# Another model of loads and of the way to TensorE in the planner that orders a diffusion trunk's instructions

## The chip, the cores and the metric

One core of one Trainium2 chip. The metric is the device time of one execution in microseconds (us); a difference is read from medians of several runs. PE is TensorE, DVE VectorE, ACT ScalarE, POOL GpSimd, SP SyncE, which issues the loads.

## The reference

A diffusion backbone of two layers over 256 latent tokens and 256 context tokens, 1024 channels wide. Each layer has four branches side by side, one output projection, and a squared-ReLU MLP; scales and shifts come from a conditioning vector (adaLN). Cut to one layer, for the latent tokens:

```python
sh1, sc1, g1, sh2, sc2, g2 = ada_mod(c, w_ada[l], b_ada[l])     # silu(c) @ w + b, split in 6
u = x * (1.0 + sc1) + sh1
p = split_proj(u @ w_in[l] + b_in[l])
y_a, y_b = local_branches(p, ...)        # 3-tap gated conv; 31-tap conv, layer norm, silu
y_c = diff_post(diff_latent(...), ...)   # differential attention: softmax1 - lam * softmax2
y_d = na_latent(..., rpb[l])             # 2-D neighbourhood attention with a position bias
y = sum_i sigmoid(gate_i) * (y_i @ wb[i] + bb[i])
x = layer_norm(ALPHA * x + g1 * (y @ w_o[l]), ...)
h = x * (1.0 + sc2) + sh2
x = layer_norm(ALPHA * x + g2 * (relu(h @ w_ff1[l]) ** 2 @ w_ff2[l]), ...)
```

The context tokens go through the same weights in layer 0; in layer 1 only their keys and values are needed.

## The kernel before

**Products.** Every weight is loaded once from HBM in units of 128 x 1024 float32, 512 KB (`raw`, 344 loads). ScalarE rounds a unit to `whi` (a copy in a shorter format, L373), VectorE makes the rest `wlo = raw - whi` (L380), and every product is three matmuls: high by high, high by low, low by high. The activations have the same two parts (`u`, `a`, `yc`, `pt`, `qk`). At the very start half units are used (`wh`, `wl`). On TensorE (L427) `mm` are the products of `u` with the input projection and with the MLP's first matrix, `f` those of the MLP's second, `br` and `wo` the branch and output projections, `S` scores, `o` attention outputs, `PT` transposes of the softmax `P` (L487), which VectorE copies to `pt`.

**The conditioning vectors.** The first ones (layer 0) are matmuls on loaded blocks `a` at the start. The others are computed while layer work runs, from about 300 to 520 us and from 680 to 960 us: `araw` units of 512 KB (80 loads) are multiplied and summed on VectorE into `sums` (L407, a unit is several instructions), TensorE adds the partitions up (`ada<-sums`), and a row `adrow` is transposed (`adT`) into `mod`. `bt` is the position bias of the neighbourhood attention (loads of 128 KB), `var` the variance of the conv branch's layer norm from sums of squares (`sum<-sum,sq`, `conf`).

**Buffers.** One pool of ten units holds at most 3 `raw`, 3 `whi`, 3 `wlo` and 2 `araw`; a load can start only when a buffer of its kind is free.

**The order.** Nothing of it is written by hand. The kernel's pieces are threads with a priority, and `Sched.run` is a list scheduler: it always takes the operation that can start first by its own clock, the higher priority among equals, and emits it to its engine's queue; `_rather` lets a more urgent one go first if it comes within a fraction of the chosen one's time. The chip's engines then execute their queues strictly in this order and wait by semaphores. The clock is made of each operation's cost and of `lat()`, the time from one engine's result to another's use (L153 to L161): 200 ns behind PE, TO_PE into PE, 128 to 205 between others. All loads are issued by SP from `dma()` (L416). In the planner a load occupies SP for its bytes over 355 per ns, at least 80 ns, and its data count as landed 2100 ns later. Operations that VectorE or ScalarE can do alike are handed out in the same step by who can start first.

Of the kernel before, what the change touches and what calls it, by code (L numbers as in the profile page):

```python
# [24 lines left out]
CAPS_S = {"qkv": 24, "P": 8, "bt": 3, "pt": 12, "y": 24}  # L25
FIRST = 5
ADA_PACE = 108
TO_PE = 300.0
MM = 13.3
PRIO_ADA = 27  # L30
PRIO_X = 60
# [9 lines left out]
LO_AFTER = {(DEPTH - 1, ("f1", 1)): ("z", DEPTH - 1, 0, 1)}  # L41
AHEAD = {"DVE": 0.3, "ACT": 0.3}
MARGIN = 20
CAPS_W = {"raw": 3, "whi": 3, "wlo": 3, "araw": 2}
CAPS_PS = {"main": 4, "att": 4, "ada": 1}
ALPHA = (2 * DEPTH) ** 0.25
# [41 lines left out]
class Buf:  # L88
    __slots__ = ("tile", "wt", "we", "rt", "re", "res")

    def __init__(self, tile, t=0.0, res=None):
        self.tile, self.wt, self.we, self.rt, self.re, self.res = tile, t, None, 0.0, None, res
# [58 lines left out]
class Sched:  # L151
    @staticmethod
    def lat(a, b):  # L153
# [5 lines left out]
        if "PE" in (a, b):  # L159
            return 200.0 if a == "PE" else TO_PE  # L160
        return 205.0 if "POOL" in (a, b) else 143.0  # L161

    def __init__(self):
        self.free = {}
        self.table = 0
        self.active = []
        self.seq = 0
        self.wake = deque()
        self.blocked = 0
# [75 lines left out]
    def _rather(self, best):  # L245
# [7 lines left out]
        for j, t in enumerate(self.active):  # L253
            if t[1] + MARGIN > prio:
                continue
# [8 lines left out]
    def run(self, everything):  # L264
        self._settle()
        while self.active:
            best = None
            for i, t in enumerate(self.active):
                op = t[3]
                for way in op[1]:  # L270
                    s = max(self.free.get(way[0], 0.0), self._ready(op, way[0]))
                    key = (s, t[1], t[2], s + way[1])
                    if best is None or key < best[0]:
                        best = (key, i, way)
            best = self._rather(best)
            (s, _, _, _), i, (eng, cost, fn, table) = best
            if eng == "PE" and s < COLD:
                cost *= 2
            if eng == "ACT" and table is not None and table != self.table:
                self.table = table  # L280
                cost += 1283.0
            t = self.active.pop(i)
            _, _, w, r, lag = t[3]
            fn()
            end = s + cost
            self.free[eng] = end
            for v in r:
                for b in v.bufs:
                    if end > b.rt:
                        b.rt, b.re = end, eng  # L290
            for v in w:
                for b in v.bufs:
                    b.wt, b.we = end + lag, eng
            self.wake.append((t, end))
            self._settle()
        if not everything.done:
            raise RuntimeError("the threads wait for each other")
# [9 lines left out]
class Kernel(Sched):  # L307
    def __init__(self, tc, es, aps):
# [7 lines left out]
        self.R = {  # L316
            "wt": Resource(big, "wt", [128, 1024], 10, CAPS_W),
            "pad": Resource(big, "pad", [128, 572], 4),
# [96 lines left out]

    def dma(self, out, in_, bytes_):  # L416
        nc, a = self.nc, self._a
        return self._op("SP", max(80.0, bytes_ / 355.0), lambda: nc.sync.dma_start(out=a(out), in_=a(in_)),
                        [out] if isinstance(out, V) else [], [in_], lag=2100.0)

    def mm(self, calls, w, r, cost):

# [1490 lines left out]
```

## Time and profile before

| | |
|---|---|
| median of 3 runs | 1617.65 us (1616.54 to 1618.89) |
| the profiled execution | 1620.5 us, of which the span from first to last instruction is 1618.7 |
| mean granted TensorE clock | 0.993 of full speed |
| PE busy | 1573.0 us, 97% |
| DVE busy | 1300.3 us, 80% |
| ACT busy | 879.6 us, 54% |
| mean DMA rate | 157 GB/s |

The rows quoted below come from the profiled execution. A row of the list of waits reads: engine, what it was about to write, its line, what ended the wait, then the sum of such waits, how many, and the longest. A row of a timeline reads: start, duration, engine, line, operation, output and inputs, size; in square brackets the idle time just before it and what ended it. A duration is longer than the distance to the next start, because instructions of an engine overlap a little. A row of stretches has each engine's busy time, then the granted clock and the DMA's share and rate.

### The profile page before, as it was taken

The numbers are of one execution on the slowest core, as the hardware profiler recorded it, in microseconds if no ns is written. First come the engines' busy times: TensorE is split into PE (matmuls) and PEld (weight loads), VectorE is DVE, ScalarE is ACT, GpSimd is POOL, SyncE is SP. The second block draws the span as 40 slices with busy tenths as digits, with TensorE's granted clock in tenths as the row PEclk, the third lists the DMA queues.
The fourth block names the chain that finished last, engine by engine and source line by source line (L and its number), as shares of the span: only waits on it lengthen the run. The fifth ranks groups of instructions, "written<-read, shape, count | busy, mean of one in ns | idle before, by whom it ended". The sixth has DMA issues, their size and how long they took to land. (4 is left out here: it accounts for less than half of the span.)

```text
span 1618.7 us, 22984 instructions
## 1 busy us (share of the span) xinstructions
PE 1573.0 (97%) x8688; PEld 1338.1 (83%) x8688; DVE 1300.3 (80%) x2192; ACT 879.6 (54%) x1425; POOL 12.5 (1%) x51
## 2 busy tenths in 40 slices
PE   7999999999999999999999999999999999989997
PEld 4878878887878888887887868888997999989997
DVE  3899999599999747987676794899999797765566
ACT  3465366455744644742523324667587686576553
POOL 0000000000000000000000000000000000000000
PEclk9999999999999999999999999999999999999999
DMA  9322222544454155455555643543443444735563
GB/s 371 112 68 83 98 79 78 166 159 152 145 191 157 65 171 193 137 195 182 188 171 184 234 147 130 177 167 106 144 151 116 144 157 166 251 131 190 192 224 110
DMA packets 80707, 254.30 MB, mean 157 GB/s; under 512 B 9028, under 2 KB 13892, under 8 KB 80596
## 3 DMA queue, kind: packets, MB, share of 16 engines
q1 hardware_dynamic: 80596, 252.84, 46.1%
q8 instruction: 68, 1.11, 0.3%
q14 instruction: 43, 0.35, 0.1%
HBM read 250.67 MB, written 2.13 MB: 156 GB/s over the span
## 5 line engine op out<-in xcount | busy, mean ns | idle before, releaser
L427 PE MATMUL mm<-u,whi 128*128 128x512 f32 (+1 forms) x3168 | 789.0, 340 | 1.5 <-ACT u L373 0.7
L427 PEld LDWEIGHTS mm<-u,whi 128*128 128x128 f32 x3168 | 547.7, 191 | 66.9 <-DVE u L380 2.4
L427 PE MATMUL mm<-u,wlo 128*128 128x512 f32 (+1 forms) x1584 | 535.5, 338 | 0.6 <-DVE wlo L380 0.6
L373 ACT ACTIVATE whi<-raw 128x1024 fp32r<-128x1024 f32 x335 | 353.8, 1057 | 332.1 <-DVE wlo L380 122.7
L380 DVE TENSOR_TENSOR wlo<-raw,whi 128x1024 fp32r<-128x1024 f32 x335 | 408.7, 1221 | 146.6 <-PE mm L427 67.5
L427 PEld LDWEIGHTS mm<-u,wlo 128*128 128x128 f32 x1584 | 302.6, 191 | 32.6 <-DVE wlo L380 0.8
L407 DVE SCALAR_TENSOR_TENSOR sums<-araw,cs,sums 128x512 f32<-128x512 f32 x280 | 195.9, 747 | 57.9 <-DMA araw<-in_w_ada 57.4
L427 PE MATMUL f<-whi,a 128*128 128x512 f32 (+1 forms) x760 | 236.7, 389 | 0.0
L427 PEld LDWEIGHTS f<-whi,a 128*128 128x128 f32 x760 | 142.3, 188 | 31.2 <-issue 2.5
L427 PE MATMUL f<-wlo,a 128*128 128x512 f32 (+1 forms) x380 | 147.5, 388 | 1.8 <-DVE wlo L380 1.8
L407 DVE SCALAR_TENSOR_TENSOR conf<-glu,sm,conf 128x512 f32<-128x512 f32 (+1 forms) x240 | 137.6, 614 | 0.8
L427 PEld LDWEIGHTS f<-wlo,a 128*128 128x128 f32 x380 | 71.4, 188 | 17.2 <-DVE wlo L380 3.2
L373 ACT ACTIVATE P<-S,st 128x512 f32<-128x512 f32 (+1 forms) x96 | 58.6, 615 | 16.4 <-DVE st L1187 15.7
L373 ACT ACTIVATE gth<-mm,hb 128x512 f32<-128x512 f32 (+1 forms) x64 | 37.0, 578 | 37.2 <-PE mm L427 37.1
L427 PE MATMUL wo<-whi,mg 128*128 128x512 f32 (+1 forms) x184 | 56.6, 382 | 0.0
L1187 DVE TENSOR_REDUCE st<-S 128x1 f32<-128x512 f32 (+1 forms) x96 | 55.0, 591 | 0.2
L427 PE MATMUL S<-qk 128*128 128x512 f32 (+1 forms) x192 | 48.7, 368 | 4.5 <-ACT qk L373 2.4
L373 ACT ACTIVATE qk<-ra 64x512 fp32r<-64x512 f32 (+1 forms) x62 | 35.0, 565 | 24.4 <-DVE ra L380 22.1
L373 ACT ACTIVATE a2f<-mm 128x512 f32<-128x512 f32 (+1 forms) x64 | 30.7, 482 | 32.0 <-PE mm L427 32.0
L373 ACT ACTIVATE bh<-br,hb 128x512 f32<-128x512 f32 (+1 forms) x64 | 36.1, 573 | 16.3 <-PE br L427 16.2
L373 ACT ACTIVATE P<-P,st 128x512 f32<-128x512 f32 (+1 forms) x42 | 26.5, 643 | 33.1 <-DVE st L1236 27.8
L380 DVE TENSOR_TENSOR a<-a2f,a 128x512 fp32r<-128x512 f32 (+1 forms) x64 | 35.4, 556 | 10.6 <-ACT a L373 9.9
(206 smaller groups left out, 1934.9 us busy)
## 6 DMA issues: line engine op xcount, KB each, us to landing
raw<-in_W SPq DMA_DIRECT2D x344, 512.0 KB
araw<-in_w_ada SPq DMA_DIRECT2D x80, 512.0 KB
a<-in_w_ada SPq DMA_DIRECT2D x32, 256.0 KB
bt<-in_rpb SPq DMA_DIRECT2D x32, 128.0 KB
row<-g SPq DMA_DIRECT2D x12, 256.0 KB
x<-in_x_t SPq DMA_DIRECT2D x8, 256.0 KB
row<-in_ln_g SPq DMA_DIRECT2D x8, 256.0 KB
row<-in_ln_b SPq DMA_DIRECT2D x8, 256.0 KB
```

What stands on the lines that cost most here:

```text
L373: lambda: nc.scalar.activation(out=out.ap, in_=in_.ap, func=func, **kw),
L380: return self._op(eng, cost, lambda: e.tensor_tensor(out=out.ap, in0=x.ap, in1=y.ap, op=op), [out], [x, y])
L407: return self._op("DVE", cost, lambda: nc.vector.scalar_tensor_tensor(out=out.ap, in0=x.ap, scalar=a(s), in1=y.ap, op0=op0, op1=op1), [out ...
L427: nc.tensor.matmul(out=out, lhsT=x, rhs=y, start=start, stop=stop, **kw)
L1187: yield self.dve(68 + 1.04 * nk, lambda: nc.vector.tensor_reduce(out=mx.ap, in_=S.ap, axis=AX.X, op=ALU.max, negate=True), [mx], [S])
```

## The change

The planner's model is changed in three numbers and two places; no operation of the kernel is. TO_PE goes from 300 to 500 ns: the planner counts a result of another engine as usable by TensorE 200 ns later than before. A load is modelled in three parts: SP is busy for 330 ns, then the bytes go one load after another through one path (`self.loads`) at 315 per ns instead of 355, then 2700 ns instead of 2100 pass until they count as landed. So in the planner SP is free for the next issue after 0.33 us, where a 512 KB load had held it for 1.48.

```diff
--- before.py
+++ after.py
@@ -25,7 +25,7 @@
 CAPS_S = {"qkv": 24, "P": 8, "bt": 3, "pt": 12, "y": 24}
 FIRST = 5
 ADA_PACE = 108
-TO_PE = 300.0
+TO_PE = 500.0
 MM = 13.3
 PRIO_ADA = 27
 PRIO_X = 60
@@ -41,6 +41,9 @@
 LO_AFTER = {(DEPTH - 1, ("f1", 1)): ("z", DEPTH - 1, 0, 1)}
 AHEAD = {"DVE": 0.3, "ACT": 0.3}
 MARGIN = 20
+DMA_LAG = 2700.0
+DMA_RATE = 315.0
+DMA_ISSUE = 330.0
 CAPS_W = {"raw": 3, "whi": 3, "wlo": 3, "araw": 2}
 CAPS_PS = {"main": 4, "att": 4, "ada": 1}
 ALPHA = (2 * DEPTH) ** 0.25
@@ -162,6 +165,7 @@
 
     def __init__(self):
         self.free = {}
+        self.loads = 0.0
         self.table = 0
         self.active = []
         self.seq = 0
@@ -282,8 +286,11 @@
             t = self.active.pop(i)
             _, _, w, r, lag = t[3]
             fn()
-            end = s + cost
-            self.free[eng] = end
+            if eng == "SP":
+                self.free[eng] = s + DMA_ISSUE
+                end = self.loads = max(s + DMA_ISSUE, self.loads) + cost
+            else:
+                end = self.free[eng] = s + cost
             for v in r:
                 for b in v.bufs:
                     if end > b.rt:
@@ -415,8 +422,8 @@
 
     def dma(self, out, in_, bytes_):
         nc, a = self.nc, self._a
-        return self._op("SP", max(80.0, bytes_ / 355.0), lambda: nc.sync.dma_start(out=a(out), in_=a(in_)),
-                        [out] if isinstance(out, V) else [], [in_], lag=2100.0)
+        return self._op("SP", bytes_ / DMA_RATE, lambda: nc.sync.dma_start(out=a(out), in_=a(in_)),
+                        [out] if isinstance(out, V) else [], [in_], lag=DMA_LAG)
 
     def mm(self, calls, w, r, cost):
```

What follows is order. TensorE and SP have as many instructions as before; VectorE has 14 more and ScalarE 14 fewer, since operations that either can do went to the other. Lines of the code below L164 stand four, those below L285 up to seven lines further down.

At the variance of the conv branch's norm (383 us in the trace of before), on TensorE, before and now:

```order
L427 MATMUL mm<-u,whi 128x512 x2
L427 MATMUL mm<-u,wlo 128x512
L427 MATMUL var<-sum,on_77 128x512
L487 MATMUL PT<-ident,P 128x128 x4
L427 MATMUL br<-yc,whi 128x512 x2
L427 MATMUL br<-yc,wlo 128x512
```

```order
L434 MATMUL mm<-u,whi 128x512 x2
L434 MATMUL mm<-u,wlo 128x512
L434 MATMUL var<-sum,on_77 128x512
L434 MATMUL mm<-u,whi 128x512 x2
L434 MATMUL mm<-u,wlo 128x512
```

`var` now stands 38 rows later on TensorE, in the midst of `mm` products; the `br` products that stood behind it are ahead of it now.

On VectorE at the same place, the last of the three sums of squares that `var` needs, before and now:

```order
L380 TENSOR_TENSOR sum<-sum,sq 128x512
L380 TENSOR_TENSOR conf<-conf,mu 128x512
L407 SCALAR_TENSOR_TENSOR gth<-gth,bh 128x512
L407 SCALAR_TENSOR_TENSOR sums<-araw,cs,sums 128x512
L380 TENSOR_TENSOR sum<-sum,sq 128x512
L380 TENSOR_TENSOR acc<-acc,gth 128x512
L380 TENSOR_TENSOR wlo<-raw,whi 128x1024
```

```order
L414 SCALAR_TENSOR_TENSOR sums<-araw,cs,sums 128x512 x2
L387 TENSOR_TENSOR wlo<-raw,whi 128x1024
L387 TENSOR_TENSOR S<-S,bt 128x256
L1194 TENSOR_REDUCE st<-S 128x1
L387 TENSOR_TENSOR sum<-sum,sq 128x512
L1243 RECIPROCAL st<-st 128x1
L394 TENSOR_SCALAR P<-P,st 128x512
```

The sum had a step of `gth` and one of `sums` just ahead of it; now it follows two `wlo`, a bias addition and a reduction, and the `sums` stand ahead of those.

On SP, the loads around the second pair of `bt` in this stretch (418 us in the trace of before), before and now:

```order
L418 DMA raw<-in_W 128x1024 x4
L418 DMA g_102<-adrow 1x512 x2
L418 DMA g_103<-adrow 1x512 x2
L418 DMA ba<-in_b_ada 128x1x512
L418 DMA araw<-in_w_ada 128x1024
L418 DMA bt<-in_rpb 128x256 x2
L418 DMA araw<-in_w_ada 128x1024 x2
L418 DMA raw<-in_W 128x1024
```

```order
L425 DMA raw<-in_W 128x1024
L425 DMA bt<-in_rpb 128x256 x2
L425 DMA raw<-in_W 128x1024 x2
L425 DMA g_102<-adrow 1x512 x2
L425 DMA g_103<-adrow 1x512 x2
L425 DMA ba<-in_b_ada 128x1x512
L425 DMA araw<-in_w_ada 128x1024 x4
L425 DMA raw<-in_W 128x1024 x2
```

The pair of `bt` stood behind the rows `g`, the bias `ba` and an `araw`; now it stands ahead of those and of two `raw`, and four `araw` stand in a row behind `ba`.

On VectorE in the MLP of layer 0, up to the `wlo` that ended at 932.67 in the trace of before and a little beyond it, before and now:

```order
L380 TENSOR_TENSOR a_8084<-a2f,a_8083 128x512
L407 SCALAR_TENSOR_TENSOR sums<-araw,cs,sums 128x512 x2
L380 TENSOR_TENSOR wlo<-raw,whi 128x1024
L407 SCALAR_TENSOR_TENSOR sums<-araw,cs,sums 128x512 x2
L380 TENSOR_TENSOR wlo<-raw,whi 128x1024
L407 SCALAR_TENSOR_TENSOR sums<-araw,cs,sums 128x512 x7
L380 TENSOR_TENSOR wlo<-raw,whi 128x1024
L407 SCALAR_TENSOR_TENSOR sums<-araw,cs,sums 128x512
L380 TENSOR_TENSOR wlo<-raw,whi 128x1024
```

```order
L387 TENSOR_TENSOR a_8062<-a2f,a_8061 128x512
L414 SCALAR_TENSOR_TENSOR sums<-araw,cs,sums 128x512 x2
L387 TENSOR_TENSOR wlo<-raw,whi 128x1024
L414 SCALAR_TENSOR_TENSOR sums<-araw,cs,sums 128x512 x5
L387 TENSOR_TENSOR wlo<-raw,whi 128x1024
L414 SCALAR_TENSOR_TENSOR sums<-araw,cs,sums 128x512 x3
L387 TENSOR_TENSOR wlo<-raw,whi 128x1024
L387 TENSOR_TENSOR yacc<-f_8036,yacc 128x512
L387 TENSOR_TENSOR yacc<-yacc,row 128x512
L414 SCALAR_TENSOR_TENSOR sums<-araw,cs,sums 128x512
```

The `wlo` in question is the one behind `sums` x7 before, and the one behind `sums` x3 now: four of the seven steps moved ahead of the `wlo` in front of it.

## Rows read from the trace of the kernel before

**Rows 1.** The page's first part: busy time of each engine, its share of the span, its instructions.

```profile
PE 1573.0 (97%) x8688; PEld 1338.1 (83%) x8688; DVE 1300.3 (80%) x2192; ACT 879.6 (54%) x1425; POOL 12.5 (1%) x51
```

**Rows 2.** The list of waits of TensorE, whole span, costliest first.

```profile
PE mm L427 <- ACT wh L373: 4.8, 2, 3.2
PE var L427 <- DVE sum L380: 3.7, 1, 3.7
...
PE ada L427 <- DVE sums L407: 2.4, 6, 0.7
...
PE f L427 <- DVE wlo L380: 1.8, 2, 1.6
PE adT L487 <- DVE adrow L380: 1.2, 2, 0.9
```

**Rows 3.** The list of waits of all engines, whole span: VectorE on loads.

```profile
DVE sums L407 <- DMA araw<-in_w_ada: 57.4, 42, 3.0
```

**Rows 4.** Busy time by stretch, from 360 to 480 us.

```profile
360.00:400.00 40.00, 36.31 (x160) 28.87 (x160) 38.19 (x62) 21.16 (x30) 0.00 (x0) 0.96 0.50 164
400.00:440.00 40.00, 40.00 (x205) 32.11 (x204) 35.71 (x64) 29.61 (x53) 0.00 (x0) 1.00 0.41 133
440.00:480.00 40.00, 37.65 (x173) 31.06 (x172) 39.29 (x64) 17.77 (x29) 0.00 (x0) 0.96 0.54 180
```

**Rows 5.** Timeline of TensorE around 383 and around 446 us.

```profile
382.51 0.62 PE L427 MATMUL mm<-u,whi 128*128 128x512 f32 x2
382.97 0.39 PE L427 MATMUL mm<-u,wlo 128*128 128x512 f32 x1
387.05 2.04 PE L427 MATMUL var<-sum,on 128*128 128x512 f32 x2 [3.69 <-DVE sum L380]
...
447.96 0.55 PE L487 MATMUL PT<-ident,P 128*128 128x128 f32 x3 [2.35 <-DVE P L387]
```

**Rows 6.** Timeline of VectorE, 369 to 388 us.

```profile
374.26 2.08 DVE L407 SCALAR_TENSOR_TENSOR sums<-araw,cs,sums 128x512 f32<-128x512 f32 x3 [0.66 <-DMA araw<-in_w_ada]
376.26 1.22 DVE L380 TENSOR_TENSOR wlo<-raw,whi 128x1024 fp32r<-128x1024 f32 x1
377.39 0.68 DVE L380 TENSOR_TENSOR conf<-conf,mu 128x512 f32<-128x512 f32 x1
...
385.03 0.69 DVE L407 SCALAR_TENSOR_TENSOR gth<-gth,bh 128x512 f32<-128x512 f32 x1
385.63 0.75 DVE L407 SCALAR_TENSOR_TENSOR sums<-araw,cs,sums 128x512 f32<-128x512 f32 x1
386.30 0.69 DVE L380 TENSOR_TENSOR sum<-sum,sq 128x512 f32<-128x512 f32 x1
```

**Rows 7.** Timeline of VectorE, 417 to 449 us.

```profile
425.48 0.43 DVE L380 TENSOR_TENSOR S<-S,bt 128x256 f32<-128x256 f32 x1 [3.10 <-DMA bt<-in_rpb]
...
447.42 0.75 DVE L387 TENSOR_SCALAR P<-P,st 128x512 f32<-128x512 f32 x2
```

**Rows 8.** Busy time by stretch, four microseconds behind each of the two waits of group 5.

```profile
448.00:452.00 4.00, 4.00 (x13) 3.19 (x14) 3.92 (x8) 1.27 (x3) 0.00 (x0) 0.57 0.48 180
...
387.00:391.00 4.00, 3.95 (x10) 2.59 (x11) 4.00 (x6) 2.13 (x3) 0.00 (x0) 0.57 0.22 68
```

**Rows 9.** Timelines of VectorE, 916 to 934 us, and of TensorE, 924 to 934 us.

```profile
924.93 2.74 DVE L407 SCALAR_TENSOR_TENSOR sums<-araw,cs,sums 128x512 f32<-128x512 f32 x4 [2.64 <-DMA araw<-in_w_ada]
929.46 2.08 DVE L407 SCALAR_TENSOR_TENSOR sums<-araw,cs,sums 128x512 f32<-128x512 f32 x3 [1.79 <-DMA araw<-in_w_ada]
931.46 1.21 DVE L380 TENSOR_TENSOR wlo<-raw,whi 128x1024 fp32r<-128x1024 f32 x1
...
932.72 0.50 PE L427 MATMUL f<-wlo,a 128*128 128x512 f32 x1 [1.63 <-DVE wlo L380]
```

**Rows 10.** Timeline of the issues on SP, 916 to 934 us.

```profile
921.18 0.33 SPq L418 DMA_DIRECT2D araw<-in_w_ada  x1
922.32 0.33 SPq L418 DMA_DIRECT2D raw<-in_W  x1
922.74 0.38 SPq L418 DMA_DIRECT2D araw<-in_w_ada  x1
```

**Rows 11.** The list of waits of all engines, 312 to 549 us.

```profile
DVE sums L407 <- DMA araw<-in_w_ada: 5.0, 9, 1.0
...
DVE S L380 <- DMA bt<-in_rpb: 3.1, 1, 3.1
...
DVE wlo L380 <- PE mm L427: 1.8, 4, 0.6
...
PE o L427 <- DVE pt L380: 0.5, 1, 0.5
```

**Rows 12.** Timeline of TensorE, 11 to 24 us.

```profile
14.77 1.22 PE L427 MATMUL mm<-u,wh 128*128 128x512 f32 x2 [3.21 <-ACT wh L373]
...
16.35 1.94 PE L427 MATMUL ada<-a,cs 128*32 128x128 f32 x32
18.21 0.83 PE L427 MATMUL mm<-u,wh 128*128 128x512 f32 x2
...
22.63 0.73 PE L427 MATMUL mm<-u,wh 128*128 128x512 f32 x2 [1.61 <-ACT wh L373]
```

**Rows 13.** Timeline of VectorE, 11 to 24 us.

```profile
15.96 0.75 DVE L380 TENSOR_TENSOR u<-uf,u 128x256 fp32r<-128x256 f32 x2
```

## The prediction

> **What bounds the kernel now.** I read the busy times first: TensorE works 1573.0 of 1618.7 us, VectorE 1300.3, ScalarE 879.6 [rows 1]. TensorE's instructions and their number are the same in both orders, so the time can only change by TensorE's idle time (and by what its clock loses behind idle). The second view is therefore what TensorE waited for [rows 2]. What is to be seen there: no wait names the load of a weight; the long ones are that of the start (4.8 for `wh`), then waits on VectorE: `var<-sum` 3.7 in one, `ada<-sums` 2.4 in six, `f<-wlo` 1.8, `adT` 1.2.
>
> The third view asks what VectorE, on which those waits stand, had itself waited for: `sums<-araw` 57.4 us in 42 waits [rows 3]. So loads that land later than the planner believed hold VectorE, whose queue is strict, and TensorE sees it only where VectorE has no slack. The fourth view, busy times by stretch, says where that is: from 360 to 480 us VectorE is busy 38.19, 35.71 and 39.29 of each 40 us [rows 4]. In 400 to 440 the 4.3 us that lack hold the 3.10 us wait for `bt` [rows 7].
>
> Two places show it. At 383.36 (382.97 + 0.39) TensorE stops for 3.69 us until 387.05, for `var` [rows 5]; VectorE was busy without a break then, and its last `sum` stood at 386.30 behind a `sums` and a `gth`, and the last of its waits for `araw` ahead of it, 0.66 at 374.26, was 12 us earlier [rows 6]. At 445.61 it stops for 2.35 us for `PT<-P` [rows 5]; the `P` at 447.42 comes 22 us after VectorE's wait of 3.10 for `bt` [rows 7]. And each of the two costs more than its length: just behind them the granted clock has a mean of 0.57 over 387 to 391 and again over 448 to 452, that is the lower level, 1.2 of 2.4 GHz, for most of each, with TensorE busy all the while [rows 8]. Work goes with the clock, so 4 us at 0.57 lose 4 x 0.43 = 1.7 us. Each wait of over two microseconds at these two places thus cost its length plus 1.7 us.
>
> **The change part by part.** Only the planner's numbers change, so nothing is added or removed on TensorE or on the load queue; the price is order alone. (VectorE gets 14 instructions more and ScalarE 14 fewer, because the planner hands out some copies by who is free.)
>
> *The load model.* Does the new model fit the loads? At 921.18 an `araw` is issued, at 922.32 a `raw`, at 922.74 a second `araw` [rows 10]; the `sums` that need the two begin at 924.93 and 929.46, each behind a wait for its load [rows 9]. So alone it took 3.75 us, behind others 6.72. The model before charges 524288/355 = 1477 ns each, one after the other, and 2100 behind: 924.8 and 922.66 + 1.48 + 1.48 + 2.1 = 927.7, so it is 1.8 us early on the second. That is the 1.79 us wait. The new one gives 330 + 1664 + 2700 = 4.69 alone (925.9, 0.9 too late, which costs nothing but a later place) and 921.51 + 3 x 1.66 + 2.7 = 929.2 on the second: 0.3 from what was seen. I expect about three quarters of VectorE's waits for loads to go.
>
> A rule of the Trainium skill speaks against this part: "DMA: Bandwidth & Descriptors", Anatomy of one DMA, gives for its path a fixed 2.0 us plus bytes/436e3. An estimate by that page is 3.2 us for 512 KB, less than even the old model's 3.58, so by it no load would be later than planned, and the time would be that of the rival below in which VectorE stays the bound. The rows above disagree (6.72 us behind others, 57.4 us of waits), so it stays a rule for a transfer alone.
>
> *312 to 549 us.* Here I took the `wlo` that starts at 312.02, the last place where both orders stand alike, and added from it the start-to-start times of each engine's instructions (227 ns for a matmul of 512 columns, from the pairs of [rows 5]; 1.13 us for a `wlo`, 0.66 for a `sums`, 0.60 for other operations of 512, from the starts in [rows 6]) up to each point where TensorE needs a result of VectorE. TensorE's lateness there is VectorE's idle time so far, plus about 0.43 us on the way, less the lead that the order gives TensorE's work over VectorE's. In the order before the lead is 70.2 - 69.8 = 0.4 at `var`, 0.2 at `PT<-P`, 1.2 at an `ada<-sums`, and -0.5 and -1.1 at two late `o<-pt`. At `var` VectorE had been idle 3.7 by then: 3.7 + 0.43 - 0.4 = 3.7, the wait seen. In the new order `var` stands after 82.9 us of TensorE work with 80.5 us of VectorE's before it, a lead of 2.4; no other point has a lead under 3 until the last two `o<-pt` products, with 0.1 and 0.0 (226.3 against 226.3).
>
> Now what goes: the waits 3.69 + 2.35 [rows 5], 0.5 at an `o<-pt` late in the stretch [rows 11], and twice 1.7 us of clock, 9.9 together. What is late next: the last `o<-pt`, by VectorE's remaining idle. That idle was 8.1 for loads in this stretch (`araw` 5.0 in nine waits, `bt` 3.1) and some 1.3 for other things (the largest group is 1.8 for `wlo` behind TensorE, a part of it after the last `o`), [rows 11]; 9.4. If three quarters of the 8.1 go, 3.3 is left, and TensorE is late by 3.3 + 0.4 = 3.7 at the last products, perhaps in several short pieces without a clock loss. Gain 9.9 - 3.7 = 6.2; I take **-6.0**. Bounds: -9.5 if no idle is left but a microsecond; 0 if all 9.4 stays, since 9.4 + 0.4 = 9.8 at the end then replaces the 9.9. The `bt` pair that VectorE waited 3.10 us for now stands on the queue of SP ahead of the last two `raw`, the `g` rows, `ba` and an `araw`, so that wait should go whatever the model is worth; what is moved behind it (those loads) is later by two issues of 0.33 us [rows 10] and two transfers of 128 KB, a quarter of the size that took 3.75 us alone; `raw` has that to spare, no wait of [rows 2] names one.
>
> *660 to 960 us.* The vectors of layer 1: `ada<-sums` 2.4, VectorE's share of `adT` 1.2 and `f<-wlo` 1.8 [rows 2], 5.4 in all, all of it between 764 and 956 us. The longest, 1.63 us before `f<-wlo` at 932.72 [rows 9], is due to the wait of 1.79 in the pair above: the `wlo` stands behind those sums. In the new order three steps of `sums` instead of seven stand between it and the `wlo` ahead, and the `ada` products stand 11 and 19 us later on TensorE at two of three places. I take **-3.5**; bounds -5 (all) and -1 (only the `wlo`'s; the third place, near 764, keeps only some 1.4 us of added room, and its sums also come later).
>
> *The start.* TensorE now takes the second step of unit 0 ahead of all eight `ada` products (four stood between before). Its first step starts at 14.77, the first `ada` at 16.35, the second step at 18.21 [rows 12]; the `u` it needs starts only at 15.96 and takes 0.75 for two [rows 13], so TensorE would wait about 0.3 us, and the `ada` chain, on which the next `wh` wait of 1.61 hangs, comes 0.86 + 0.3 later. VectorE and ScalarE each put one more `u` ahead of the next `wl` and `wh`. I take **+1.0**, bounds 0 and +1.5.
>
> *The rest.* From 80 to 300 us the smallest leads are alike in both orders, from 968 to 1230 VectorE's and TensorE's orders are alike, and the chain that ends in the transposes ahead of the last MLP too; 0, give or take 1.5. The added margin ahead of TensorE costs nothing of itself: it decides places, no instruction waits for it.
>
> Sum: -6.0 - 3.5 + 1.0 = -8.5. The profiled execution took 1620.5 us, so 1612.0 for it; it lies 2.85 above the median 1617.65, which goes to **1609**.
>
> **The rivals.** *All load waits of VectorE go:* for it speaks that the new model came within 0.3 us of the pair. The stage gives -9.5, the later one -5, the start +0.5: -14, 1604. Against it: the loads of one stretch share a path with all others, and a stage near saturation makes new waits.
> *VectorE stays the bound from 312 to 549:* its 9.4 us of idle only change place, because `araw` has two buffers and each can be loaded only when its last `sums` is done, in whatever order. Then TensorE waits the 9.8 at the last `o<-pt`; stage 0, the later stage -2, start +1: -1, 1617. The rule of the skill's page above, if it held here, would end in this case. Against it: the leads grew by 2 to 3 us along the whole stretch, so that short waits are absorbed.
> *Slower: loads in bunches.* The new order of SP issues `araw` in pairs and fours near 418 and 450, where single ones alternated with `raw`. A second one of a pair cost VectorE 1.79 us of waiting at 929.46 [rows 9]. If none of the 8.1 us goes and four pairs each add 1.79, 7.2 us more, the last `o<-pt` is late by 17, the stage costs +7.2; with +1.0 at the start and -3.5 later, +4.7: 1622. It decides from the point where bunches add over 2.5 + 3.2 us, that is from a fourth pair. Against it: a bunch waits at issue for its buffers, so most pairs are no pairs on the path.
> *That the order does nothing* cannot be: rows change on every engine.
>
> **How the numbers follow.** A difference under 0.2% (3.2 us) is no difference here. Forecast (1605 to 1614): 0.56; all load waits go (under 1605): 0.12; VectorE stays the bound (1614.4 to 1620.9): 0.20; bunches: 0.12. So faster 0.68, same 0.20, slower 0.12. The range has to hold eight in ten: 1603, just past the first rival, to 1619.5, past the middle of the second.
>
> **What would show it.** Right: the `var` and `PT<-P` waits gone from TensorE's list and the clock at 1.0 around 387 and 448; VectorE's `sums<-araw` waits down from 57.4 to 15 or 20; TensorE's next waits at the last `o<-pt` near 540, under 4 us; `f<-wlo` gone near 931; the first 34 us longer by a microsecond. Wrong: `sums<-araw` still above 40, or a wait of over 5 us (with a fall of the clock) at an `o<-pt`, or a new wait on `wlo` or `whi` behind a late `raw`, which the list before does not have.

## The result and the profile after

The changed kernel takes 1598.93 us (median of 4 runs, 1597.91 to 1599.84) against 1617.1 us before in the same runs: a ratio of 0.9892 with a 95% interval of 0.987 to 0.9914. It is faster by 18 us, where 8.5 had been forecast; the time lies below the stated range. The profiled execution took 1597.91 us, its span is 1596.0.

The page's first part, against [rows 1]:

```profile
PE 1560.8 (98%) x8688; PEld 1336.3 (84%) x8688; DVE 1306.3 (82%) x2206; ACT 870.5 (55%) x1411; POOL 12.4 (1%) x51
```

TensorE executes the same 8688 matmuls and is busy 12.2 us less. That is the first thing to see: more than half of the 22.7 us by which the span fell left the column that counts as work, and the forecast had looked only at idle time.

The list of waits of TensorE (against [rows 2]) and, under it, of VectorE on loads (against [rows 3]), both over the whole span:

```profile
PE ada L434 <- DMA a<-in_w_ada: 5.6, 4, 3.9
PE mm L434 <- ACT wh L380: 5.1, 2, 3.2
PE uT L494 <- DVE r L394: 3.2, 1, 3.2
PE o L434 <- DVE pt L387: 2.0, 2, 1.8
...
DVE sums L394 <- DMA araw<-in_w_ada: 12.4, 5, 6.6
DVE sums L414 <- DMA araw<-in_w_ada: 12.1, 7, 3.4
```

`var`, the long `PT<-P`, `ada<-sums`, `f<-wlo` and VectorE's share of `adT` are gone from the first list. VectorE's 42 waits of `sums` for `araw`, 57.4 us, became 7 of 12.1; the first step of a sum (L394) waits a little more.

Where the time went is read by looking up the same product, the n-th of its name, in both timelines. Differences of after against before by stretch of before:

| stretch of before, us | forecast | measured |
|---|---|---|
| start to 43 | +1.0 | +1.05 |
| 43 to 314 | 0 | -1.36 |
| 314 to 557 | -6.0 | -5.57 |
| 557 to 698 | 0 | -1.32 |
| 698 to 1043 | -3.5 | -14.14 |
| 1043 to the end | 0 | -1.37 |
| sum | -8.5 | -22.71 |

(The profiled execution of before, 1620.5 us, is one of the longer of its runs; the medians differ by 18.2.) Two of the three priced stretches came out within half a microsecond of the forecast number; whether for its reasons is told further below. The third holds 10.6 us more than forecast.

Busy time by stretch, 360 to 480 us, against [rows 4], and the two places of [rows 8], then the four microseconds behind the wait for `o<-pt`:

```profile
360.00:400.00 40.00, 40.00 (x174) 32.40 (x173) 38.11 (x57) 19.98 (x28) 0.00 (x0) 1.00 0.54 177
400.00:440.00 40.00, 40.00 (x212) 32.68 (x211) 39.67 (x67) 28.33 (x47) 0.00 (x0) 1.00 0.45 147
440.00:480.00 40.00, 39.76 (x188) 32.80 (x187) 39.74 (x70) 22.60 (x41) 0.00 (x0) 1.00 0.56 183
387.00:391.00 4.00, 4.00 (x19) 3.34 (x18) 4.00 (x7) 2.15 (x3) 0.00 (x0) 1.00 0.41 136
448.00:452.00 4.00, 4.00 (x19) 3.32 (x18) 4.00 (x7) 1.64 (x2) 0.00 (x0) 1.00 0.85 280
...
537.00:541.00 4.00, 3.58 (x15) 2.91 (x16) 3.15 (x9) 2.09 (x5) 0.00 (x0) 0.52 0.00 0
```

TensorE no longer stops in the first two stretches, VectorE is at 39.67 and 39.74 of 40 in the other two, and the clock is at 1.0 where it had been 0.57. What is late next is what the forecast named: the last `o<-pt`, 1.80 us at 536.94, with a fall of the clock behind it (0.52, mostly the 1.2 GHz level). From the list of all engines' waits, 312 to 549 us, the largest of VectorE's on ScalarE between 312 us and that stop, and what is left of its waits for loads there:

```profile
DVE gth L414 <- ACT gth L380: 2.2, 2, 1.3
...
DVE sums L414 <- DMA araw<-in_w_ada: 0.4, 2, 0.2
```

The start, timeline of TensorE, against [rows 12]; under it the place in before that the row at 26.31 has to be held against:

```profile
14.91 1.22 PE L434 MATMUL mm<-u,wh 128*128 128x512 f32 x2 [3.21 <-ACT wh L380]
...
16.36 1.34 PE L434 MATMUL mm<-u,wh 128*128 128x512 f32 x2
...
18.06 2.06 PE L434 MATMUL ada<-a,cs 128*32 128x128 f32 x64
...
22.78 0.73 PE L434 MATMUL mm<-u,wh 128*128 128x512 f32 x2 [1.92 <-ACT wh L380]
...
26.31 1.08 PE L434 MATMUL ada<-a,cs 128*32 128x128 f32 x32
...
34.56 0.50 PE L434 MATMUL mm<-u,wl 128*128 128x512 f32 x1 [1.05 <-DVE wl L387]
```

```profile
26.34 1.08 PE L427 MATMUL ada<-a,cs 128*32 128x128 f32 x32
```

At 26.3 us both orders are level. The microsecond is lost at 34.56, behind a `wl` that VectorE makes 1.29 us later than before: the `adT` whose result VectorE takes ahead of it starts at 32.78 instead of 32.13, and the `wl` now stands behind the steps `G` and `uf` too. Before and then after:

```profile
32.53 1.29 DVE L380 TENSOR_TENSOR wl<-raw,wh 128x512 fp32r<-128x512 f32 x2
```

```profile
33.82 1.29 DVE L387 TENSOR_TENSOR wl<-raw,wh 128x512 fp32r<-128x512 f32 x2
```

Now the stretch that was mispriced. Around one of its three groups of `ada` products (eight products, each of them two matmul rows in the trace; such a row is called a pass here), TensorE in before and, under it, in after:

```profile
855.48 3.02 PE L427 MATMUL ada<-sums,ones 128*32 128x512 f32 x10
858.78 1.05 PE L427 MATMUL ada<-sums,ones 128*32 128x512 f32 x4 [0.28 <-DVE sums L407]
860.57 1.04 PE L427 MATMUL ada<-sums,ones 128*32 128x512 f32 x2 [0.74 <-DVE sums L407]
861.55 0.50 PE L427 MATMUL f<-whi,a 128*128 128x512 f32 x1
```

```profile
857.37 1.94 PE L434 MATMUL ada<-sums,ones 128*32 128x512 f32 x16
859.24 0.74 PE L434 MATMUL mm<-u,whi 128*128 128x512 f32 x2
```

Sixteen passes took 6.07 us (855.48 to 861.55) and take 1.87 (857.37 to 859.24). Of the 4.2 us lost, the list of TensorE's waits shows 0.28 + 0.74 and a few hundredths. The rest, some 3 us, is no idle time. In after the passes start four at a time and lie on top of one another. In before the late sums cut the group into pieces of eight, two, four and two passes, which run one behind another, and a piece of two takes as long as one of four (1.04 and 1.05). A pass counts as busy up to its modelled end, so such a piece looks as busy as a whole group. The weight loads don't hide it. TensorE's weight loads in before, the same place, and VectorE's chain ahead of it:

```profile
855.48 0.14 PEld L427 LDWEIGHTS ada<-sums,ones 128*32 128x32 f32 x4 [0.35 <-DVE sums L407]
...
857.45 0.14 PEld L427 LDWEIGHTS ada<-sums,ones 128*32 128x32 f32 x2 [0.97 <-DVE sums L407]
858.77 0.14 PEld L427 LDWEIGHTS ada<-sums,ones 128*32 128x32 f32 x4 [1.19 <-DVE sums L407]
860.57 0.14 PEld L427 LDWEIGHTS ada<-sums,ones 128*32 128x32 f32 x2 [1.65 <-DVE sums L407]
```

```profile
852.41 2.74 DVE L407 SCALAR_TENSOR_TENSOR sums<-araw,cs,sums 128x512 f32<-128x512 f32 x4 [2.73 <-DMA araw<-in_w_ada]
856.64 2.08 DVE L407 SCALAR_TENSOR_TENSOR sums<-araw,cs,sums 128x512 f32<-128x512 f32 x3 [1.49 <-DMA araw<-in_w_ada]
858.64 1.22 DVE L380 TENSOR_TENSOR wlo<-raw,whi 128x1024 fp32r<-128x1024 f32 x1
859.77 0.74 DVE L407 SCALAR_TENSOR_TENSOR sums<-araw,cs,sums 128x512 f32<-128x512 f32 x1
```

VectorE waited 2.73 and 1.49 us for two loads, and its last sum ended at 860.51; TensorE had been in the group since 855.48. Waits of the weight loads over 680 to 985 us, before and then after, and the busy time of the ten microseconds around the group in both:

```profile
PEld ada L427 <- DVE sums L407: 9.6, 9, 1.7
```

```profile
PEld ada L434 <- DVE sums L414: 1.1, 3, 0.4
```

```profile
853.00:863.00 10.00, 8.91 (x34) 3.62 (x32) 8.51 (x13) 2.12 (x2) 0.00 (x0) 1.00 0.48 165
```

```profile
853.00:863.00 10.00, 10.00 (x54) 6.94 (x53) 7.65 (x12) 4.09 (x6) 0.00 (x0) 1.00 0.39 140
```

8.91 of 10 busy, but 34 matmuls where the other kernel does 54: the count and the 3.62 of PEld say what the busy share doesn't. The three groups of the stretch last, from first to last start of a pass, 2.54, 5.55 and 5.71 us in before and 1.34 or 1.35 each after: 9.8 us. With the listed waits for `adT` (1.2) and `f<-wlo` (1.8) that is 12.8 of the 14.1; held product against product, the rest stands at the same places, and nothing is won between them.

### The profile page after: what moved, and what is told of

Same layout as the page of the kernel before. It is cut to its first block, busy times and chain, and to the rows that moved or that the text cites. A ratio compares the mean times of both kernels' runs of the same rounds, so it can differ in the third digit from the quotient of the medians.

```text
span 1596.0 us, 23002 instructions
## 1 busy us (share of the span) xinstructions
PE 1560.8 (98%) x8688; PEld 1336.3 (84%) x8688; DVE 1306.3 (82%) x2206; ACT 870.5 (55%) x1411; POOL 12.4 (1%) x51
## 4 chain that ended last, share of the span: by engine, by line
PE 58%; DVE 8%; ACT 1%; issue 1%; POOLq 0%; POOL 0%; DVEq 0%; ACTq 0%
PE mm L434 29%; PE f L434 16%; PE wo L434 4%; PE br L434 4%; DVE wlo L387 2%; DVE conf L414 1%; PE nv L434 1%; PE o L434 1%; PE dv L434 1%; PE PT L494 1%; DVE qk L387 1%; DVE st L1194 1%; PE S L434 0%; DVE pt L387 0%; PE uT L494 0%
## 5 line engine op out<-in xcount | busy, mean ns | idle before, releaser
L414 DVE SCALAR_TENSOR_TENSOR sums<-araw,cs,sums 128x512 f32<-128x512 f32 x280 | 195.2, 745 | 12.5 <-DMA araw<-in_w_ada 12.1
L434 PE MATMUL S<-qk 128*128 128x512 f32 (+1 forms) x192 | 48.5, 367 | 3.7 <-ACT qk L380 1.2
L380 ACT ACTIVATE qk<-ra 64x512 fp32r<-64x512 f32 (+1 forms) x67 | 37.7, 563 | 22.7 <-DVE ra L387 21.4
L434 PE MATMUL dv<-whi,u 128*128 128x512 f32 x128 | 43.3, 398 | 0.5 <-ACT P L380 0.5
```

The source lines that it names most:

```text
L380: lambda: nc.scalar.activation(out=out.ap, in_=in_.ap, func=func, **kw),
L414: return self._op("DVE", cost, lambda: nc.vector.scalar_tensor_tensor(out=out.ap, in0=x.ap, scalar=a(s), in1=y.ap, op0=op0, op1=op1), [out ...
L434: nc.tensor.matmul(out=out, lhsT=x, rhs=y, start=start, stop=stop, **kw)
```

## Experiments

The theory after reading this: the gain comes from loads being planned to land later, so that VectorE meets landed data; the margin TO_PE adds little. The rival: the margin is the active part. Differences by stretch, of the profiled executions against that of before (us; the last column is the whole). Each row is a single execution, and the runs of before alone lie between 1612.5 and 1623.5 us, so small differences in it show nothing:

| kernel | to 43 | 43 to 314 | to 557 | to 698 | to 1043 | to the end | span |
|---|---|---|---|---|---|---|---|
| after | +1.05 | -1.36 | -5.57 | -1.32 | -14.14 | -1.37 | -22.71 |
| e1_margin | -1.13 | -0.73 | -0.07 | -1.35 | -0.46 | -0.46 | -4.20 |
| e2_loads | +3.11 | -0.77 | -6.29 | -1.35 | -13.43 | +0.68 | -18.05 |
| e3_landing | +1.83 | -1.00 | -4.68 | -1.34 | -13.09 | -0.86 | -19.14 |
| e4_issue | -0.21 | -0.86 | -6.05 | -1.31 | -2.28 | +0.03 | -10.68 |
| e7_adalater | +1.83 | -0.52 | -1.25 | -1.33 | +4.41 | -0.47 | +2.67 |
| e10_together | -0.96 | -0.13 | +1.76 | -1.34 | +2.04 | +0.64 | +2.01 |
| e11_araw | -0.34 | -0.50 | -9.56 | +0.05 | -14.14 | -1.28 | -25.77 |
| e12_others | +1.19 | -1.01 | -6.87 | -0.10 | -0.48 | -1.71 | -8.98 |
| e13_araw_margin | +1.03 | -0.78 | -4.73 | -1.34 | -10.14 | -0.20 | -16.16 |

**e1_margin**, only the margin:

```diff
 # the kernel before, and
-TO_PE = 300.0
+TO_PE = 500.0
```

> The changed kernel with the load model of before (SP held for bytes/355, landing 2100 ns later) and only TO_PE at 500. Theory: the gain of 18 us comes from later landing of loads in the plan, the margin alone moves the ada products no later behind their sums, so the stretch from 690 to 1000 us keeps its loss of 14 us and the stretch from 312 to 549 its 5.6: 1613 to 1618 us, ratio to before 0.997 to 1.001. Rival: the margin alone gives VectorE's results the room that TensorE lacked: half the gain or more, 1599 to 1608 us, ratio under 0.994.

1614.7 us (10 runs), ratio 0.998 [0.9965, 0.9995]. As the theory said: VectorE's `sums` still wait 55.9 us for `araw`, and both long stretches keep their loss.

**e2_loads**, only the load model:

```diff
 # the changed kernel, and
-TO_PE = 500.0
+TO_PE = 300.0
```

> The changed kernel with TO_PE back at 300, only the load model new. Theory: nearly all of the gain, ratio 0.988 to 0.993 (1598 to 1606 us), with the stretch 690 to 1000 us shorter by 13 to 14 us and var and the long PT wait gone. Rival (the margin is what counts): ratio 0.994 to 1.0.

1600.44 us, ratio 0.9892 [0.9869, 0.9915], the same as with the margin. The load model is the change.

**e3_landing**, of the load model only the two numbers:

```diff
 # the kernel before, and
-        return self._op("SP", max(80.0, bytes_ / 355.0), ..., lag=2100.0)
+        return self._op("SP", max(80.0, bytes_ / 315.0), ..., lag=2700.0)
```

> The kernel before with two numbers changed: bytes/315 and a landing 2700 ns later; SP is still held for the whole transfer in the plan, TO_PE 300. Theory: late landing is the active part of the load model, so the sums and the ada products behind them move back and most of the gain comes: ratio 0.990 to 0.995. Rival (the short issue on SP, which lets loads go out earlier, is the active part): ratio 0.996 to 1.001.

1600.59 us, ratio 0.9891 [0.9869, 0.9913]. The later landing alone gives all of it.

**e4_issue**, of the load model only its structure:

```diff
 # the changed kernel, and
-TO_PE = 500.0
+TO_PE = 300.0
-DMA_LAG = 2700.0
-DMA_RATE = 315.0
+DMA_LAG = 2100.0
+DMA_RATE = 355.0
```

> The kernel before with the short issue of 330 ns and one shared path, but the old numbers 355 and 2100; TO_PE 300. Theory: loads go out earlier, but the sums are still planned too early; the ada products stand where they stood (within 1.5 us of work), so the stretch 690 to 1000 us loses 10 us or more against the changed kernel: ratio 0.996 to 1.002. Rival (short issue is the active part): ratio 0.989 to 0.994.

1608.34 us, ratio 0.9938 [0.9914, 0.9962]: over half of the gain, and by the median just inside the rival's range, with an interval that reaches into the theory's. By stretch each has its part. That of 698 to 1043 keeps nearly all its loss, as the theory said, but 314 to 557 gains 6.05 without any later landing. So the two stretches have different needs: the first is mended by issuing earlier or by planning later, the second only by planning later. VectorE, whole span:

```profile
DVE sums L414 <- DMA araw<-in_w_ada: 48.5, 30, 2.8
```

The next two ask what exactly cost TensorE the 14 us. Theory A: it lost time only where it met late sums, inside the groups.

**e7_adalater**, groups later in the plan, loads as before:

```diff
 # the kernel before, and, for the ada products on sums,
-                              [*sums[2 * h], *sums[2 * h + 1], self.ones], 1000)
+                              [*sums[2 * h], *sums[2 * h + 1], self.ones], 1000) + (ADA_LATE,)   # 8000 ns more until ready
```

> The kernel before, old load model and TO_PE 300; only the ada products on sums are counted as ready 8 us later in the plan. Theory: the 14 us between 690 and 1000 us were TensorE held inside the three ada groups by sums that came late, so moving the groups back is enough: that stretch shorter by 10 to 12 us (its f<-wlo waits stay), although VectorE still waits for araw 50 us or more; 1604 to 1609 us, ratio 0.992 to 0.995. Rival (VectorE's waits for loads were what mattered, by all that they held back): the stretch shorter by 4 us or less, ratio 0.997 to 1.0.

1617.72 us, ratio 1.0004 [0.9991, 1.0016]: nothing gained (its profiled execution, 1623.15, is the slowest of its ten, so its row of the table is not typical). It doesn't decide, because the edit also tore the two halves of each group apart (878.83 and 883.66 in one of them), and each half took 1.84 us, as much as a whole group. So:

**e10_together**, the same for the first half only:

```diff
-                              [*sums[2 * h], *sums[2 * h + 1], self.ones], 1000) + (ADA_LATE,)
+                              [*sums[2 * h], *sums[2 * h + 1], self.ones], 1000) + (() if h else (ADA_LATE,))
```

> The kernel before with only the first half of each ada group counted as ready 8 us later in the plan, so that the two halves stay together (in e7_adalater they came apart and each half took 1.8 us). The groups now stand 6 to 9 us of TensorE work later. Theory A (late sums cost TensorE time only where it meets them, in the groups): the three late groups take 1.34 us from first to last start and the stretch 697 to 982 us gets 9 to 11 us shorter; 1606 to 1609 us, ratio 0.992 to 0.995. Theory B (VectorE is late by its waits for loads, and what stands behind the sums in its queue, the wlo, is the next thing that TensorE meets): the groups are whole too, but f<-wlo waits rise from 1.8 to 6 us or more, the stretch gains 5 us or less; 1612 to 1617 us, ratio 0.996 to 1.0.

1623.83 us, ratio 1.0037 [1.0024, 1.0049]. The groups are whole, 1.34 us each from first to last start, no wait for sums is left on TensorE in this stretch, and nothing is gained: it is 6 us slower, more than either theory had given. TensorE's waits from 680 to 985 us, then VectorE's:

```profile
PE adT L488 <- DVE adrow L381: 5.0, 2, 3.7
PE mm L428 <- DVE wlo L381: 3.1, 3, 1.3
PE f L428 <- DVE wlo L381: 2.5, 3, 1.1
```

```profile
DVE sums L408 <- DMA araw<-in_w_ada: 50.7, 34, 3.2
```

Theory A fell. B stands in the main, though not in its detail (`f<-wlo` is at 2.5, where 6 or more had been expected): 10.6 us of waits behind other results of VectorE, where before has 3.0, took the place of the loss in the groups. The loss belongs to VectorE, which stands 50.7 us for loads in a strict queue; where TensorE meets it is a matter of order.

**e11_araw** and **e12_others** split the later landing by load:

```diff
 # the kernel before, and
+        rate, lag = (315.0, 2700.0) if araw else (355.0, 2100.0)      # e11_araw; e12_others: if not araw
 # (left out: the lines that use rate and lag, and that mark the loads of araw)
```

> The kernel before, with the later landing (bytes/315 and 2700 ns) for the loads of araw alone; all other loads, the structure of the model and TO_PE as before. Theory: the sums behind araw are what was planned too early, so this has most of what the later landing of all loads gave (17 us in e3_landing): 1600 to 1606 us, ratio 0.989 to 0.993. Rival (the weights' landing matters, through wlo): ratio 0.995 to 1.0.

> The kernel before, with the later landing for all loads except araw. Theory: sums are planned as early as before, VectorE waits for araw 45 us or more, and the late groups stay torn: 1611 to 1618 us, ratio 0.996 to 1.0. Rival (the weights' landing matters): ratio 0.989 to 0.993.

e11_araw: 1596.26 us (1594.23 to 1598.74), ratio 0.9865 [0.9848, 0.9882]. e12_others: 1617.39 us, ratio 0.999 [0.9974, 1.0005] (its profiled execution, 1611.5, is the fastest of its ten, so its row of the table is not typical); its three late groups stay torn, 4.35, 4.51 and 6.58 us from first to last start. VectorE in e11_araw and e12_others, whole span:

```profile
DVE sums L407 <- DMA araw<-in_w_ada: 20.0, 15, 2.8
```

```profile
DVE sums L407 <- DMA araw<-in_w_ada: 53.1, 37, 2.9
```

(The first steps of the sums wait 16.6 and 12.1 us more.) e11_araw is faster than even the theory expected. What counts is where the sums stand in VectorE's queue. With the weights' landing as before, the stretch to 1043 us is as short as with all loads late (-14.14), and the one to 557 shorter still. e11_araw's median is the best measured here, 2.7 us below the changed kernel, whose interval overlaps with its own.

**e13_araw_margin** adds the margin to that:

```diff
 # e11_araw, and
-TO_PE = 300.0
+TO_PE = 500.0
```

> e11_araw (later landing for araw alone) with TO_PE at 500 as in the changed kernel. Theory: the margin alone was worth 3 us in e1_margin, where VectorE's results were late; with the sums in place there is little left for it: 1593 to 1599 us, ratio to before 0.985 to 0.988. Rival (the two add up): 1590 to 1593, ratio 0.983 to 0.985; or the margin only shuffles the order: 1599 to 1604.

1603.0 us, ratio 0.9909 [0.9894, 0.9925]: 7 us slower than e11_araw. The last of the three cases: on top of a good order the margin only makes another one, which loses at 314 to 557 and after 698, where the groups are torn again (2.82, 4.76 and 1.91 us from first to last start). So not every order that lands `araw` later is a good one. The margin is worth -3 us on the old model, nothing that can be told on the new one (e2_loads against after), +7 here.

**e5_quarters** was to price the overlap of the products in a group:

```diff
 # the changed kernel, and, in the order of a group's products,
-for c in range(2) for q in (2 * h, 2 * h + 1)], [ps],
+for q in (2 * h, 2 * h + 1) for c in range(2)], [ps],
```

> The changed kernel with the eight products of each ada group in another order on TensorE: the two of one quarter of the output directly behind each other, instead of alternating between two quarters; all waits stay met. It prices what TensorE loses if products of different quarters can't overlap. Theory (the four microseconds per group in the kernel before were waits for sums, not lost overlap): a group grows from 1.8 to between 2.7 and 3.5 us, five groups add 4 to 8 us, 1603 to 1607. Rival (lost overlap is the larger part of it): a group grows to 6 us or more, five add 20: 1618 to 1622. No effect at all: 1599.

1599.08 us, ratio 0.9879 [0.9864, 0.9894]: no effect, the case given as "no effect at all". A group still takes 1.35 us from first to last start. The order of the products in the queue doesn't matter as long as all four quarters are there. So this order took no overlap away, and the run can't say what lost overlap costs; that is seen in the torn group of before above and in the half groups of e7_adalater.

**e8_lag3300** and **e9_start** try for more:

```diff
 # the changed kernel, and e8_lag3300:
-DMA_LAG = 2700.0
+DMA_LAG = 3300.0
 # or e9_start: while the plan's clock is under 40 us, SP held for bytes/355 and landing 2100 ns later
```

> The changed kernel with loads counted as landed 3300 ns after their transfer instead of 2700. Theory: the waits that later landing removes are gone at 2700, so what is left of VectorE's waits for araw (24 us) may fall to 10 without moving TensorE: 1597 to 1603 us, ratio to before 0.987 to 0.992. Rival (every microsecond of VectorE's waits is worth part of one): 1590 to 1595.

> The changed kernel with the load model of before for the first 40 us of the plan and the new one behind it. Theory: the new model costs 1 us at the start (in the profile 1.05, where the margin with the old model gains 1.1), and the rest of the order stays as in the changed kernel: 1 to 3 us faster than it, 1596 to 1598 us, ratio to before 0.985 to 0.988. Rival: another start moves the later order and gives it back, 1599 to 1603.

e8_lag3300: 1601.41 us, ratio 0.9896 [0.9881, 0.991], so the effect is used up at 2700. e9_start: 1598.95 us, ratio 0.9879 [0.9862, 0.9895], the changed kernel's own time. +1.06 at 43 us is unchanged, although its list has no wait for `wl`; some 2.5 us won by 123 us are partly given back by 314, and what was won is lost again where the clock stayed up in after (-0.02 instead of -1.32 before 698). The time falls on the rival's edge (1599), and another start did move the later order, as it said.

## Why two stretches came out near the forecast and the third did not

- **The load model.** That the new one comes within 0.3 us of the second load of a pair, where the old one is 1.8 early, was the reason for expecting three quarters of VectorE's waits to go (for the first load the old one is nearer, 0.2 early against 0.9 late). Of 57.4 us, 45 went; with the first steps of the sums it is 67.0 that became 24.5. Shown as the cause by e2_loads and e3_landing, and that `araw` is the load that counts by e11_araw and e12_others.
- **312 to 549 us.** -6.0 forecast, -5.57 measured; `var` and `PT<-P` gone with their falls of the clock, the last `o<-pt` the next to be late, as written. That the number came so near is in part luck. VectorE's waits of over 0.15 us from 312 us up to that stop sum up to 3.2 us, where 3.3 had been forecast, but 0.4 of it is for loads (2.0 forecast) and 2.8 for results of ScalarE (1.3 forecast, of any kind). And the 3.7 us of lateness, hoped for without a clock loss, came as 1.80 us of waiting and a fall of the clock (0.52 over 537 to 541, still 0.50 over 541 to 543).
- **The start.** +1.0 forecast, +1.05 measured, but the number was right by luck. The forecast put it on the second step's `u` and on the `ada` chain behind it; the `ada` products did begin at 18.06 instead of 16.35, and the wait for `wh` grew from 1.61 to 1.92, yet at 26.3 us nothing of it was left. The microsecond is the wait of 1.05 for `wl` at 34.56, which the forecast did not have. That some of it was won back by 126 us (the wait of 0.88 for `S<-qk` at 92 us is gone) was not foreseen.
- **660 to 960 us, the step that failed.** "5.4 in all" took TensorE's loss from the list of its matmuls' waits, and "bounds -5 (all)" made that the most there was to win. The loss was 14.1: the same list for weight loads has 9.6 us for sums in this stretch, where the matmuls' list has 2.4, and both rows are of the trace of before. The mechanism (late `araw`, late sums, `ada`, `adT` and `f<-wlo` behind them) was right; the term was mis-sized, above all its 2.4 for `ada`, which was 9.8, since late sums also keep the passes of a group from running side by side. It alone put the time below the range: with -14.1 in its place the sum is -19.1, which gives 1598.6.
- **The rest.** "0, give or take 1.5" was -4.05 in the profile, of which 1.3 stands near 677 us, where the clock fell in before (0.66 over 676 to 680) and not in after (1.00 over 672 to 676). Nine of the twelve other orders did the same, e1_margin, e7_adalater and e10_together among them, so it is no merit of the new model; in the three others (e9_start, e11_araw, e12_others) the clock falls there too, to 0.66, 0.62 and 0.57 over four microseconds, and why it does so in these stays open.
- **The rivals.** That all load waits go (1604) was the nearest, on the side given 0.12, but by its time alone: 24.5 us of those waits are left, and what carried the time there is the mis-sized term. VectorE staying the bound (1617) and the bunches of loads (1622) did not come. The bound of -9.5 in the stretch of 312 to 549 is what its rule gives for no idle at all; with a microsecond left it is 9.9 - 1.4 = 8.5.
- **A reading.** "No wait names the load of a weight" is wrong: the costliest row of TensorE's list in before is `PE ada L427 <- DMA a<-in_w_ada: 5.4, 5, 3.8`, loads of conditioning weights at the start. It is 5.6 after, so nothing hung on it.

## What to carry to other kernels

Read the waits of TensorE's weight loads beside those of its matmuls: a stretch that is 89% busy can do 34 matmuls where 54 fit. The Trainium skill, "Perfetto Trace Analysis", Identifying the Most-Contended Engine, calls matmul busy time no good measure of how near TensorE is to its limit and takes, beside the work done, the weight loads' busy share; this trace agrees, with 3.62 against 6.94 of 10 us. When an engine with a strict queue waits for loads, price its own waiting: moving the place where TensorE meets it (e10_together) only moves the wait, and planning the readers of those loads later (e11_araw) wins back what TensorE lost by it. A planner's load time has to be long enough for the loads whose readers stand in that queue (2700 and 3300 ns did alike); for the others alone it made no difference here (e12_others). And a number that comes out right has to be looked up in the trace like one that does not: of the two stretches that fitted, one did so by another wait than the forecast's.

## What the runs showed of the hardware

Products that write different quarters of 32 output rows go side by side: in a whole `ada` group four passes start within 0.04 us, and the next four 0.43 us later, so 16 passes take 1.87 us; a half group of 8 passes takes 1.84 (e7_adalater), because only two lie side by side. The Trainium skill's "TensorE: Matmul & The Clock Gate", Part 3, tells of such overlap of small products at different tile positions; the trace agrees. New to me was that their order in the queue is free: with both products of one quarter directly behind each other (e5_quarters) a group takes the same 1.35 us from first to last start.

Kernels whose sums wait for loads seem to spread more from run to run: before from 1614.15 to 1623.53 in 13 runs, e1_margin 1611.59 to 1619.27, e12_others 1611.5 to 1621.62, against 1599.78 to 1602.45 for e2_loads and 1599.86 to 1601.34 for e3_landing. But these two have four runs each, and e4_issue, whose sums wait 48.5 us, stays between 1606.1 and 1609.83 in four runs, so the connection is not shown.
